# Latent attention: where the softmax is divided, and one norm chain for keys and queries

## Chip, cores and metric

One core of a Trainium2 chip runs the whole program. The metric is device time in microseconds from one launch; the kernel before was timed three times, and one further execution was profiled.

## What is computed

Two decoder blocks over 512 tokens of width 1024. The change lies in the second block's latent attention: 16 heads, of which each query and each key has 64 parts without and 32 parts with rotation. All four kinds are normalised by their mean square:

```python
c_kv = rms_norm_2(ckv[..., :KV_LORA_RANK], kv_a_norm)
k_rope = apply_rope(rms_norm_2(ckv[..., KV_LORA_RANK:], k_rope_norm), cos, sin)
kv = (c_kv @ w_kv_b).reshape(bsz, seq, N_HEADS, QK_NOPE_DIM + V_DIM)
k_nope = rms_norm_2(kv[..., :QK_NOPE_DIM], k_nope_norm)
...
q_nope = rms_norm_2(q[..., :QK_NOPE_DIM], q_nope_norm)
q_rope = apply_rope(rms_norm_2(q[..., QK_NOPE_DIM:], q_rope_norm), cos, sin)
...
s = jnp.einsum('bhqd,bhkd->bhqk', q_blk, k).astype(jnp.float32) * scale
s = jnp.where(key_pos[None, :] <= query_pos[:, None], s, NEG_INF)
p = jax.nn.softmax(s, axis=-1).astype(v.dtype)
return jnp.einsum('bhqk,bhkd->bhqd', p, v)
...
x = x + o @ mla_w_o[j]
```

## The kernel before

Every product of float32 matrices is made of three passes (`passes`): each operand is split into a high and a low part (`split`: ScalarE writes the high part, VectorE or GpSimd the rest).

The method `mla` works on four groups of four heads. For each group it makes keys (`k0` to `k3`), queries (`q0` to `q3`), values (`v0` to `v3`) and the output projection (`o0` to `o3`) in the order of `HEADS_ORDER`; these parts are generators, and after every step of attention the main loop takes as many pieces of them as `MLA_PACE` and `MLA_PIECES` say, so that projections of the next group run beside the attention of this one. `mla_tokens` projects keys or queries into `tok` (tokens on partitions), sums their squares into `m_ssq`, makes the factors `hs_s` by a chain of small VectorE instructions (`hs_m`, `rq_a`, `rq_y`), scales the 64 parts on GpSimd and the 32 parts on VectorE, and rotates the queries' 32 parts with `rope`. Keys get a copy of the one rotated key part, `krope`.

The attention has 32 units: for each head two units of two blocks of 128 queries. `mla_qk` transposes queries and keys of a head; `mla_probs` makes a unit's scores in PSUM (`ps_z`), adds the mask `wide` and takes the maximum in one VectorE instruction (`a_mx`), multiplies the maximum by minus the scale, lets ScalarE take the exponential with the sum (`a_sm`), and multiplies each row of probabilities `mp` by the reciprocal of its sum, one block on VectorE and one on GpSimd. Four units later (`MLA_AHEAD`) `mla_turn` transposes the probabilities on TensorE and splits them (`pth`, `ptl`), and after both heads of a pair `mla_out` calls `pair_out`: products with the values (`ps_s`), of which the upper 64 partitions hold what the values' low parts give, so that ScalarE copies them to `t`, VectorE adds the two halves of each head, and the result is split into `os`.

Engines take their instructions in a fixed order, set when the program is built; semaphores make one wait for another. PSUM has two banks for `ps_d` (projections), two for `ps_z`, three for `ps_p` (transposes) and one for `ps_s`. The tiles `t` have three buffers.

Of the kernel before, what the change touches and what calls it, by code (L numbers as in the profile page):

```python
# [16 lines left out]
P = 128  # L17
T = 512
# [30 lines left out]
MLA_PIECES = dict(k=7, q=7, v=5, o=8)  # L49
# [9 lines left out]
def shape_constants():  # L59
# [14 lines left out]
    wide[:, 3 * P:4 * P] = np.where(c > r, -BIG, 0.0)  # L74
# [55 lines left out]
class Kern:  # L130
# [104 lines left out]
    def pair_out(self, hi, lo, n, v, p):  # L235
# [60 lines left out]
    GUESS = {1: 0x5E82C800, 32: 0x6102C800}  # L296
# [84 lines left out]
    def load_constants(self):  # L381
# [21 lines left out]
        self.pad(self.cp, 16)  # L403
# [986 lines left out]
    def rope_tables(self):  # L1390
# [11 lines left out]
        for nm in ("q", "k"):  # L1402
            g = self.row(nm + "_rope")
            t = self.cp.tile([P, 4, 4, 16], F32, name="rope_" + nm)
            for i, (src, half) in enumerate(((w[2], 0), (w[1], 1), (w[1], 0), (w[2], 1))):
                gb = g[:, half * 16:half * 16 + 16].unsqueeze(1).to_broadcast(sh)
                self.tt(t[:, i], src, gb, ALU.mult)
# [3 lines left out]
    def rope(self, out, x, tab, sh):  # L1411

        n = math.prod(sh[1:])
        t = [self.tmp() for _ in range(-(-n // 128))]
        names = "abcd"[:len(sh) - 1]
        dims = {c: s for c, s in zip(names, sh[1:])}
        per = T // n
        t = [t[i // per][:, i % per * n:(i % per + 1) * n].rearrange(
            f"p ({' '.join(names)}) -> p {' '.join(names)}", **dims) for i in range(4)]
# [37 lines left out]
    def mla(self, x):  # L1457
# [21 lines left out]
        for c in range(4):  # L1479
# [5 lines left out]
        self.rope(krope, krt, lambda i: tabs["k"][:, i], [P, 4, 16])  # L1485
# [5 lines left out]
        copy_k = lambda x: nc.gpsimd.tensor_copy(out=x, in_=krope.unsqueeze(2).to_broadcast([P, 4, 4, 32]))  # L1491
        tab_q = lambda i: tabs["q"][:, i].unsqueeze(2).to_broadcast([P, 4, 4, 16])
        make = dict(k=lambda t: self.mla_tokens(t, st, lat["kv"], 64, copy_k),
                    v=lambda t: self.mla_values(t, st, lat["kv"]),
# [360 lines left out]
```

## Time and profile before

| what | value |
|---|---|
| three runs | 2255.79, 2259.34, 2263.17 us; median 2259.34 |
| profiled execution | 2261.87 us, span of the trace 2260.0 us |
| busy share of the span | TensorE 96%, VectorE 63%, ScalarE 44%, GpSimd 12% |
| mean granted TensorE clock | 0.981 of full speed |
| latent attention with its lead-in | about 1600 to 1890 us |

The names of engines in rows are PE (TensorE matmuls), PEld (its loads of weights), DVE (VectorE), ACT (ScalarE), POOL (GpSimd). An instruction of a helper has the helper's line: L205 is any two-operand VectorE or GpSimd instruction, L209 one with scalars, L212 one with a scalar and two operands, L215 any ScalarE instruction, L231 any matmul of `passes`; tiles tell them apart. A busy TensorE is not TensorE at its peak, since matmuls are pipelined.

### The profile page before, as it was taken

To read this page: it belongs to the slowest core of one execution; us is meant where nothing else is said; L and a number is where in the kernel's file an instruction comes from. 1 tells how busy PE (TensorE), PEld (TensorE's weight loads), DVE (VectorE), ACT (ScalarE), POOL (GpSimd) and SP (SyncE) were. 2 spreads that over 40 slices of the span, in tenths; PEclk is the share of its full clock that TensorE was granted. 3 is DMA by queue.
4 is the path that set the end of the run, shared out by engine and by line. 5 is a ranking of instruction groups with operands and counts; after the bars stand their busy time and mean duration, and the time that the engine had idled before them with its cause. 6 is when DMAs were issued, how large, how long until landed. Compare 5 with 4: busy or idle time off the path is not lost.

```text
span 2260.0 us, 28842 instructions
## 1 busy us (share of the span) xinstructions
PE 2161.9 (96%) x10586; PEld 1808.0 (80%) x10586; DVE 1416.0 (63%) x2778; ACT 1001.7 (44%) x1902; POOL 278.1 (12%) x308
## 2 busy tenths in 40 slices
PE   8998999999999999998789999999988999999999
PEld 7777878887888888887668788888777877888887
DVE  6678756667667656657884554354579886543542
ACT  5443346666444545454223432233467655432331
POOL 4123201111000000000440000000025441000000
PEclk9999999999999999999899999999999999999999
DMA  4211123235423343443663233232220111323322
GB/s 153 88 48 38 33 90 111 98 117 173 149 84 104 124 152 126 146 150 123 208 208 107 85 98 98 94 103 93 82 65 32 47 37 58 101 94 95 101 93 93
DMA packets 86829, 231.60 MB, mean 102 GB/s; under 512 B 10016, under 2 KB 19744, under 8 KB 86688
## 3 DMA queue, kind: packets, MB, share of 16 engines
q1 hardware_dynamic: 74016, 208.60, 28.5%
q10 hardware_dynamic: 12672, 21.16, 3.0%
q8 instruction: 83, 1.36, 0.2%
q14 instruction: 58, 0.48, 0.1%
HBM read 202.46 MB, written 27.26 MB: 102 GB/s over the span
## 4 chain that ended last, share of the span: by engine, by line
PE 81%; DVE 11%; ACT 3%; issue 2%; DMA 2%; POOL 1%; SPq 0%; ACTq 0%; DVEq 0%; POOLq 0%
PE ps_d L231 68%; PE ps_p L263 3%; PE ps_p L231 3%; PE ps_z L231 2%; PE ps_s L243 1%; DVE t L205 1%; DVE wlo L205 1%; PE ps_s L263 1%; DMA matB<-s5m 1%; PE ps_p L848 1%; ACT sb_e L215 1%; DVE h L212 0%; DVE s5t L205 0%; DVE mp L1646 0%; DVE tok L205 0%
## 5 line engine op out<-in xcount | busy, mean ns | idle before, releaser
L231 PE MATMUL ps_d<-h,whi 128*128 128x512 f32 (+1 forms) x3152 | 996.5, 393 | 9.9 <-DVE t L205 5.1
L215 ACT ACTIVATE whi<-wraw 128x512 fp32r<-128x512 f32 (+1 forms) x648 | 403.0, 625 | 722.4 <-PE ps_d L231 638.7
L231 PEld LDWEIGHTS ps_d<-h,whi 128*128 128x128 f32 (+1 forms) x3152 | 591.8, 189 | 134.5 <-ACT whi L215 4.9
L205 DVE TENSOR_TENSOR wlo<-wraw,whi 128x512 fp32r<-128x512 f32 x585 | 409.5, 703 | 381.2 <-ACT whi L215 375.8
L231 PE MATMUL ps_d<-h,wlo 128*128 128x512 f32 (+1 forms) x1576 | 620.3, 394 | 4.9 <-DVE wlo L205 4.9
L231 PEld LDWEIGHTS ps_d<-h,wlo 128*128 128x128 f32 (+1 forms) x1576 | 297.3, 189 | 66.9 <-DVE wlo L205 6.6
L231 PE MATMUL ps_d<-fh,whi 128*128 128x512 f32 x608 | 237.3, 390 | 0.0
L231 PE MATMUL ps_d<-fl,whi 128*128 128x512 f32 x608 | 237.0, 390 | 0.0
L231 PE MATMUL ps_d<-fh,wlo 128*128 128x512 f32 x608 | 236.6, 389 | 0.0
L205 DVE TENSOR_TENSOR t<-ps_d,rsb 128x512 f32<-128x512 f32 x136 | 92.9, 688 | 127.1 <-PE ps_d L231 124.2
L231 PEld LDWEIGHTS ps_d<-fl,whi 128*128 128x128 f32 x608 | 114.1, 188 | 23.7
L231 PEld LDWEIGHTS ps_d<-fh,wlo 128*128 128x128 f32 x608 | 114.2, 188 | 23.6
L231 PEld LDWEIGHTS ps_d<-fh,whi 128*128 128x128 f32 x608 | 114.1, 188 | 23.1
L205 POOL TENSOR_TENSOR wlo<-wraw,whi 128x512 fp32r<-128x512 f32 (+3 forms) x63 | 78.4, 1249 | 107.1 <-ACT whi L215 106.9
L215 ACT ACTIVATE fh<-t 128x512 fp32r<-128x512 f32 x76 | 47.9, 631 | 63.2 <-DVE t L205 54.4
L205 DVE TENSOR_TENSOR fl<-t,fh 128x512 fp32r<-128x512 f32 x76 | 52.6, 692 | 32.8 <-ACT fh L215 30.7
L231 PE MATMUL ps_d<-whi,c 128*128 128x256 f32 (+1 forms) x224 | 55.3, 331 | 12.5 <-DVE v L212 10.2
L1645 POOL MEMSET mp<- 128x128 f32 x32 | 6.6, 209 | 461.1 <-PE ps_d L231 444.8
L231 PEld LDWEIGHTS ps_d<-whi,c 128*128 128x128 f32 x224 | 39.7, 201 | 15.7 <-DVE v L212 11.6
L231 PE MATMUL ps_d<-os,whi 128*128 128x512 f32 x128 | 47.9, 428 | 4.1 <-ACT os L215 2.1
L215 ACT ACTIVATE t<-ps_d 128x512 f32<-128x512 f32 (+1 forms) x42 | 25.1, 597 | 58.3 <-PE ps_d L231 58.0
L205 DVE TENSOR_TENSOR x<-ps_d,x 128x512 f32<-128x512 f32 x56 | 38.3, 688 | 15.8 <-PE ps_d L231 15.6
(406 smaller groups left out, 3254.7 us busy)
## 6 DMA issues: line engine op xcount, KB each, us to landing
wraw<-in_w_gu SPq DMA_DIRECT2D x88, 512.0 KB, 3.3
wraw<-in_w_ff SPq DMA_DIRECT2D x64, 512.0 KB, 3.3
wraw<-in_w_dn SPq DMA_DIRECT2D x44, 512.0 KB, 3.4
wraw<-in_w_gates SPq DMA_DIRECT2D x24, 512.0 KB, 3.4
wraw<-in_w_glu SPq DMA_DIRECT2D x16, 512.0 KB, 3.3
wraw<-in_w_sc SPq DMA_DIRECT2D x12, 512.0 KB, 3.4
gsc<-t SPq DMA_DIRECT2D x24, 256.0 KB, 2.0
sg<-gsc SPq DMA_DIRECT2D x24, 256.0 KB, 3.5
```

What stands on the lines that cost most here:

```text
L205: self.note((eng or self.nc.vector).tensor_tensor(out=out, in0=a, in1=b, op=op))
L215: self.note(self.nc.scalar.activation(out, a, fn, **kw))
L231: self.note(self.nc.tensor.matmul(ps, lhsT=a, rhs=b, start=(start and n == 0), stop=(stop and n == 3 * len(ops) - 1), skip_group_check=loose))
L243: self.note(self.nc.tensor.matmul(o, lhsT=v(h, j), rhs=x, start=(j == 0 and i == 0), stop=(j == n - 1 and i == 1)))
L263: self.nc.tensor.matmul(ps, lhsT=lhsT, rhs=rhs, start=start, stop=stop)
L848: self.nc.tensor.matmul(self.sb_at(z, i), lhsT=self.tri if j == i else self.neg, rhs=self.sb_at(s, j), start=False, stop=(j == i and n == ...
L1645: nc.gpsimd.memset(p[b][:, c0 + n:c0 + n + P], 0.0)
```

## The change

Three things are done differently. (1) The queries' gain holds minus the scale (`qgain`), the mask is positive, and a row's least value is taken in place of its greatest, so that it is the bias of the exponential as it stands. (2) Probabilities are not divided. The sums of a pair of heads and two query blocks are kept in one tile; in `pair_out` VectorE takes the reciprocal of each sum spread over 64 columns, TensorE transposes that twice into a bank of `ps_p`, and VectorE multiplies the heads' outputs by it. (3) The latent's own norm factor no longer multiplies the head norms; it becomes an offset (`mla_offs`) of the mean square. Keys and queries of a group are first only projected (`mla_raw`), and one chain of 48 columns then serves both. The rotation takes two products over all 32 parts, where it had four over 16. `MLA_PIECES`, pads and tables follow.

```diff
-MLA_PIECES = dict(k=7, q=7, v=5, o=8)
+MLA_PIECES = dict(k=5, q=8, v=5, o=8)
...
-    wide[:, 3 * P:4 * P] = np.where(c > r, -BIG, 0.0)
+    wide[:, 3 * P:4 * P] = np.where(c > r, BIG, 0.0)
...
         self.act(s[0:64], po[64:128])
+        if sums is not None:
+            rc = self.tmp()[:, 0:256].rearrange("p (a h n) -> p a h n", a=2, h=2)
+            self.nc.vector.reciprocal(out=rc, in_=sums.unsqueeze(3).to_broadcast([P, 2, 2, 64]))
+            pr = self.ps("p")
+            for a in range(2):
+                self.nc.tensor.transpose(pr[:, a * P:(a + 1) * P], rc[:, a].rearrange("p h n -> p (h n)"), self.ident)
         y = self.tmp()[:, 0:256]
         for h in range(2):
             hs = slice(h * 256, h * 256 + 256)
             self.tt(y[h * 64:h * 64 + 64], po[0:64, hs], s[0:64, hs], ALU.add)
+        if sums is not None:
+            self.tt(y, pr[:, 0:256], y, ALU.mult)
         self.split(hi, lo, y)
...
-        x1, x2 = x[..., 0:16], x[..., 16:32]
-        self.tt(t[0], x1, tab(0), ALU.mult)
-        self.tt(t[1], x2, tab(1), ALU.mult)
-        self.tt(t[2], x1, tab(2), ALU.mult)
-        self.tt(t[3], x2, tab(3), ALU.mult)
-        self.tt(out[..., 0:16], t[0], t[1], ALU.subtract)
-        self.tt(out[..., 16:32], t[2], t[3], ALU.add)
+        t = [self.tmp()[:, 0:n].rearrange(f"p ({' '.join(names)}) -> p {' '.join(names)}", **dims) for _ in range(2)]
+        for i in range(2):
+            self.tt(t[i], x, tab(i), ALU.mult)
+        self.tt(out[..., 0:16], t[0][..., 0:16], t[0][..., 16:32], ALU.subtract)
+        self.tt(out[..., 16:32], t[1][..., 0:16], t[1][..., 16:32], ALU.add)
...
+        self.ts(self.qgain, self.col("qk_q"), -1.0 / math.sqrt(96), ALU.mult)
+        self.mla_offset(0, lat["kv"][1])
+
+        def make_k(g):
+            self.ssq = self.tmp("m_ssq", shape=[P, 3, 4, 4])
+            yield from self.mla_raw(heads[g]["k"], st, lat["kv"], 64, [self.ssq[:, 0]])
+
+        def make_q(g):
+            ssq = self.ssq
+            yield from self.mla_raw(heads[g]["q"], st, lat["q"], 96, [ssq[:, 1], ssq[:, 2]])
+            yield from self.mla_tokens(heads[g]["k"][0], heads[g]["q"][0], ssq, krope, tab_q)
...
+    def mla_offset(self, i, scale):
+        self.nc.vector.reciprocal(out=self.offs[:, i], in_=scale[1])
+        self.ts(self.offs[:, i], self.offs[:, i], 64 * EPS, ALU.mult)
+
+    def mla_raw(self, head, st, latent, nq, ssq):
...
+            for (lo, hi), out in zip(parts, ssq):
+                self.nc.vector.tensor_reduce(out=out[:, c, :], in_=sq[:, :, lo:hi], axis=AX.X, op=ALU.add)
             yield
+        head.append(tok)
+
+    def mla_tokens(self, k, q, ssq, krope, tab_q):
+        nc = self.nc
+        wide = lambda t, n: t.unsqueeze(3).to_broadcast([P, n, 4, 4])
+        m = self.tmp("hs_m", shape=[P, 3, 4, 4])
+        self.tt(m[:, 0:2], ssq[:, 0:2], wide(self.offs, 2), ALU.add)
+        self.stt(m[:, 2:3], ssq[:, 2:3], 2.0, wide(self.offs[:, 1:2], 1), ALU.mult, ALU.add)
+        y = self.rsqrt(m.rearrange("p i c h -> p (i c h)"), (P, 48), "h", k=8).rearrange(
+            "p (i c h) -> p i c h", i=3, c=4)
+        scaled = lambda i, w: y[:, i].unsqueeze(3).to_broadcast([P, 4, 4, w])
+        nc.gpsimd.tensor_copy(out=k[:, :, :, 64:96], in_=krope.unsqueeze(2).to_broadcast([P, 4, 4, 32]))
         yield
+        x = q[:, :, :, 64:96]
+        self.tt(x, x, scaled(2, 32), ALU.mult)
+        self.rope(x, x, tab_q, [P, 4, 4, 32])
         yield
+        for i, t in enumerate((k, q)):
+            x = t[:, :, :, 0:64]
+            self.tt(x, x, scaled(i, 64), ALU.mult, nc.gpsimd)
+        yield
...
             nc.vector.tensor_tensor_reduce(out=p[b][:, cs], in0=z[b][:, cs], in1=wide[:, 4 * P - n:], scale=1.0,
-                                           scalar=-3e38, op0=ALU.add, op1=ALU.max, accum_out=mx[:, a:a + 1])
-        self.ts(mx, mx, -sc, ALU.mult)
+                                           scalar=3e38, op0=ALU.add, op1=ALU.min, accum_out=mn[:, a:a + 1])
         for a, (b, cs) in enumerate(cols):
-            self.act(p[b][:, cs], p[b][:, cs], AF.Exp, scale=sc, bias=mx[:, a:a + 1], accum_out=sm[:, a:a + 1])
-        nc.vector.reciprocal(out=sm, in_=sm)
-        for a, (b, cs) in enumerate(cols):
-            self.ts(p[b][:, cs], p[b][:, cs], sm[:, a:a + 1], ALU.mult, eng=nc.gpsimd if a else None)
+            self.act(p[b][:, cs], p[b][:, cs], AF.Exp, scale=-1.0, bias=mn[:, a:a + 1], accum_out=sums[a])
         return p
```

The first place is on VectorE, where the second output tile of the first group is put together (`t<-ps_s,t` adds the halves). Before:

```order
L1651 RECIPROCAL a_sm<-a_sm 128x2
L1577 TENSOR_REDUCE m_ssq_15177<-tm 128x4
L209 TENSOR_SCALAR mp<-mp,a_sm 128x384
L205 TENSOR_TENSOR t<-ps_s,t 64x256 x2
L212 SCALAR_TENSOR_TENSOR qkl<-ps_p,cols,qkh 96x512
L205 TENSOR_TENSOR os<-t,os 128x256
```

and after:

```order
L249 RECIPROCAL t<-a_sm 128x256
L205 TENSOR_TENSOR t<-ps_s,t 64x256 x2
L1594 TENSOR_REDUCE m_ssq<-tm 128x4
L205 TENSOR_TENSOR t<-ps_p,t 128x256
L1594 TENSOR_REDUCE m_ssq<-tm 128x4
L212 SCALAR_TENSOR_TENSOR qkl<-ps_p,qgain,qkh 96x512
L205 TENSOR_TENSOR os<-t,os 128x256
```

The reciprocal of 256 columns stands directly ahead of the additions, and a product with the transposed reciprocals follows them.

The second place is on TensorE, at the third pair of query blocks and heads: projections for the next group (`ps_d<-whi,c`), scores (`ps_z`) and the transposes of the next unit's probabilities (`ps_p<-cst,mp`). Before:

```order
L231 MATMUL ps_d<-whi,c 128x384 x2
L231 MATMUL ps_d<-wlo,c 128x384
L231 MATMUL ps_z<-qkh 128x384
L231 MATMUL ps_z<-qkh,qkl 128x384
L231 MATMUL ps_z<-qkl,qkh 128x384
L231 MATMUL ps_z<-qkh 128x512
L231 MATMUL ps_z<-qkh,qkl 128x512
L231 MATMUL ps_z<-qkl,qkh 128x512
L1665 MATMUL ps_p<-cst,mp 128x128 x8
```

and after:

```order
L231 MATMUL ps_d<-whi,c 128x384 x2
L231 MATMUL ps_d<-wlo,c 128x384
L252 MATMUL ps_p<-cst,t 128x128 x2
L1680 MATMUL ps_p<-cst,mp 128x128 x8
L231 MATMUL ps_z<-qkh 128x384
```

The transposes of the reciprocals (L252) are new and stand right ahead of those of the probabilities, and the scores that stood ahead of these now stand behind them.

The third place is on GpSimd, around the scaling of the second group's keys and queries. Before, with the products of the probabilities between:

```order
L1491 COPY tok<-krope 128x16x32
L205 TENSOR_TENSOR wlo<-wraw,whi 128x384 x2
L1645 MEMSET mp 128x128
L209 TENSOR_SCALAR mp<-mp,a_sm 128x256
L1645 MEMSET mp 128x128
L209 TENSOR_SCALAR mp<-mp,a_sm 128x256
L205 TENSOR_TENSOR tok<-tok,hs_s_14909 128x16x64
```

and after:

```order
L1608 COPY tok<-krope 128x16x32
L205 TENSOR_TENSOR wlo<-wraw,whi 128x384 x2
L1664 MEMSET mp 128x128
L205 TENSOR_TENSOR tok<-tok,rq_yh 128x16x64 x2
L1664 MEMSET mp 128x128 x2
```

The products of the probabilities are gone, and the scalings of keys and queries stand next to each other.

## Rows read from the trace of the kernel before

**Rows 1.** Page, part 1: busy us, share of the span, instructions

```profile
PE 2161.9 (96%) x10586; PEld 1808.0 (80%) x10586; DVE 1416.0 (63%) x2778; ACT 1001.7 (44%) x1902; POOL 278.1 (12%) x308
```

**Rows 2.** Stretches: us, busy PE, PEld, DVE, ACT, POOL (count), clock, DMA, GB/s

```profile
1675.00:1885.00 210.00, 185.24 (x1125) 162.71 (x1126) 183.51 (x549) 137.67 (x337) 98.30 (x102) 0.93 0.12 39
1736.00:1760.00 24.00, 18.37 (x121) 16.31 (x120) 23.65 (x81) 15.40 (x39) 13.19 (x14) 1.00 0.06 17
1799.00:1816.00 17.00, 12.68 (x84) 10.91 (x83) 16.31 (x47) 11.41 (x27) 9.65 (x10) 0.90 0.20 62
```

**Rows 3.** Chain of waits, 1675 to 1885 us, shares by line

```profile
by line: PE ps_d L231 25.0%; PE ps_z L231 10.6%; PE ps_s L243 6.5%; DVE mp L1646 5.1%; DVE t L205 5.1%; DVE tok L205 4.9%; DVE ptl L205 4.8%; PE ps_p L1665 4.5%; PE ps_p L1613 3.9%; ACT mp L215 3.6%; issue 2.8%; DVE v L212 2.3%; DVE a_mx L2
```

**Rows 4.** Waits, 1680 to 1885 us: total us, times, longest

```profile
PE ps_d L231 <- DVE v L212: 9.4, 5, 3.1
DVE a_sm L1651 <- ACT mp L215: 3.6, 6, 1.3
```

**Rows 5.** VectorE groups, 1640 to 1900 us: busy us, mean ns | idle before

```profile
L209 DVE TENSOR_SCALAR mp<-mp,a_sm 128x384 f32<-128x384 f32 x16 | 8.1, 505 | 0.2
L209 DVE TENSOR_SCALAR mp<-mp,a_sm 128x128 f32<-128x128 f32 x16 | 5.0, 313 | 0.1
L209 DVE TENSOR_SCALAR a_mx<-a_mx 128x2 f32<-128x2 f32 x32 | 9.5, 298 | 0.1
L1651 DVE RECIPROCAL a_sm<-a_sm 128x2 f32<-128x2 f32 x32 | 5.3, 165 | 4.1 <-ACT mp L215 3.6
L212 DVE SCALAR_TENSOR_TENSOR hs_m<-m_ssq,ls_q 128x16 f32<-128x16 f32 x8 | 3.1, 408 | 0.0
L209 DVE TENSOR_SCALAR hs_m<-hs_m 128x32 f32<-128x32 f32 x4 | 2.6, 640 | 0.1
L212 DVE SCALAR_TENSOR_TENSOR rq_yh<-rq_ah,rq_yh 128x32 f32<-128x32 f32 x8 | 1.5, 188 | 0.1
L205 DVE TENSOR_TENSOR t<-tok,rope_q 128x256 f32<-128x256 f32 x16 | 6.4, 456 | 0.0
L205 DVE TENSOR_TENSOR x<-ps_d,x 128x512 f32<-128x512 f32 x32 | 21.7, 687 | 3.3 <-PE ps_d L231 3.1
L205 DVE TENSOR_TENSOR os<-t,os 128x256 fp32r<-128x256 f32 x16 | 6.6, 420 | 2.9 <-ACT os L215 2.9
L205 DVE TENSOR_TENSOR tok<-tok,hs_s 128x512 f32<-128x512 f32 x4 | 8.8, 2190 | 0.0
```

**Rows 6.** VectorE's other reciprocals, whole span

```profile
L474 DVE RECIPROCAL beta<-g_e 128x16 f32<-128x16 f32 x1 | 0.3, 253 | 0.0
L1117 DVE RECIPROCAL small<-small 128x32 f32<-128x32 f32 x1 | 0.4, 353 | 0.0
```

**Rows 7.** Timeline, GpSimd and VectorE: start us, us, what

```profile
1714.43 1.90 POOL L205 TENSOR_TENSOR tok<-tok,hs_s 128x1024 f32<-128x1024 f32 x1
1714.63 2.24 DVE L205 TENSOR_TENSOR tok<-tok,hs_s 128x512 f32<-128x512 f32 x1
```

**Rows 8.** GpSimd groups, 1640 to 1900 us

```profile
L209 POOL TENSOR_SCALAR mp<-mp,a_sm 128x512 f32<-128x512 f32 x16 | 26.4, 1651 | 18.0 <-DVE a_sm L1651 13.7 <-DVE a_mx L209 2.5 <-PE ps_d L231 1.7
L209 POOL TENSOR_SCALAR mp<-mp,a_sm 128x256 f32<-128x256 f32 x16 | 15.7, 981 | 22.3 <-DVE a_sm L1651 8.5 <-PE ps_d L231 4.9 <-DVE rq_yh L209 3.8
```

**Rows 9.** Chain of waits in order of time: start us, us, what

```profile
1736.80 0.43 DVE t L205
1774.67 1.42 ACT mp L215 x4
1795.44 3.16 PE ps_d L231 x18
1867.69 0.87 PE ps_p L1665 x8
1881.53 0.42 DVE t L205
```

**Rows 10.** TensorE's transposes of the probabilities, 1675 to 1885 us

```profile
L1665 PE MATMUL ps_p<-cst,mp 128*128 128x128 f32 x192 | 29.4, 272 | 0.0
```

More of the change, by code (lines that the diff above doesn't have):

```diff
@@ L233, in passes, with pair_out @@
                 n += 1
-    def pair_out(self, hi, lo, n, v, p):
+    def pair_out(self, hi, lo, n, v, p, sums=None):
         po = self.ps("s")
@@ L1490, in mla @@
         heads = [{} for _ in range(4)]
[L1491 to L1494, printed above, removed]
-                    q=lambda t: self.mla_tokens(t, st, lat["q"], 96, lambda x: self.rope(x, x, tab_q, [P, 4, 4, 16])))
+        tab_q = lambda i: tabs["q"][:, i].unsqueeze(2).to_broadcast([P, 4, 4, 32])
+        self.ts(self.qgain, self.col("qk_q"), -1.0 / math.sqrt(96), ALU.mult)
[7 more added lines that the diff above has]
+            yield from self.mla_tokens(heads[g]["k"][0], heads[g]["q"][0], ssq, krope, tab_q)
+        make = dict(k=make_k, q=make_q, v=lambda g: self.mla_values(heads[g]["v"], st, lat["kv"]))
         order = iter(HEADS_ORDER)
@@ L1503, in more @@
                 else:
-                    t = heads[g][part[0]] = []
-                    yield from make[part[0]](t)
+                    heads[g][part[0]] = []
+                    yield from make[part[0]](g)
                     yield
@@ L1525, in mla @@
                     qk[l % 2] = self.mla_qk(l, heads[g]["q"][0], heads[g]["k"][0])
-                live[n] = self.mla_probs(u, qk[l % 2], wide)
+                if l % 2 == 0:
+                    sums[l // 2, u] = self.tmp("a_sm", shape=(P, 2, 2), bufs=4)
+                live[n] = self.mla_probs(u, qk[l % 2], wide, [sums[l // 2, u][:, a, l % 2:l % 2 + 1] for a in range(2)])
             if n >= MLA_AHEAD:
@@ L1532, in mla @@
                 if l % 2:
-                    self.mla_out(l // 2, u, pt, heads[g]["v"], outs[g][l // 2])
+                    self.mla_out(l // 2, u, pt, heads[g]["v"], outs[g][l // 2], sums.pop((l // 2, u)))
                     pt = []
@@ L1559, in token_major @@
             yield c, o
-    def mla_tokens(self, head, st, latent, nq, rot):
-        nc = self.nc
-        cl, (r, r2) = latent
+    def mla_offset(self, i, scale):
+        self.nc.vector.reciprocal(out=self.offs[:, i], in_=scale[1])
+        self.ts(self.offs[:, i], self.offs[:, i], 64 * EPS, ALU.mult)
+    def mla_raw(self, head, st, latent, nq, ssq):
         tok = self.pool.tile([P, 4, 4, 96], F32, name="tok", tag="tok", bufs=4)
-        parts = [(0, 64)] if nq == 64 else [(0, 64), (64, 96)]
-        n = len(parts)
-        sh = [P, n, 4, 4]
-        ssq = self.tmp(f"m_ssq{n}", shape=sh)
-        for c, ps in self.token_major(st, cl, 4 * nq):
+        parts = [(0, 64), (64, 96)][:len(ssq)]
+        for c, ps in self.token_major(st, latent[0], 4 * nq):
             self.act(tok[:, c, :, 0:nq], ps.rearrange("p (h n) -> p h n", n=nq))
@@ L1609, in mla_qk @@
         qk = []
-        for src, gcol in ((q, "qk_q"), (k, "qk_k")):
+        for src, gc in ((q, self.qgain), (k, self.col("qk_k"))):
             pt = self.ps("p")
@@ L1624, in mla_place, with mla_probs @@
         return [(0, 0), (u, 256 * (1 - u))]
-    def mla_probs(self, u, qk, wide):
+    def mla_probs(self, u, qk, wide, sums):
         nc = self.nc
         (qh, ql), (kh, kl) = qk
-        sc = 1.0 / math.sqrt(96)
         nb = u + 1
@@ L1669, in mla_turn, with mla_out @@
         return hl
-    def mla_out(self, pair, u, hl, V, o):
+    def mla_out(self, pair, u, hl, V, o, sums):
         hi, lo = (t[:, u * 256:u * 256 + 256] for t in o)
@@ L1675, in mla_out @@
         self.pair_out(hi, lo, 2 * u + 2, lambda h, j: V[j][:, (2 * pair + h) * P:(2 * pair + h + 1) * P],
-                      lambda h, j: [at(t, j) for t in hl[h][j // 2]])
+                      lambda h, j: [at(t, j) for t in hl[h][j // 2]], sums)
     def dump_blocks(self, name, tiles):
```

46 lines of the change are left out of this document (12 added, 34 removed).

## Prediction

> **What bounds the kernel now.** I read the page first: TensorE is busy 96% of the span, VectorE 63% [rows 1], so anything that does not keep TensorE waiting is worth nothing. Then the busy times by stretch. The latent attention's pipelined part, 1675 to 1885 us, is the only place that the change touches in quantity, and there the reader sees another picture: TensorE 185.2 of 210 us, VectorE 183.5, ScalarE 137.7, GpSimd 98.3, granted clock 0.93 [rows 2]. In two stretches around the norms of the next heads VectorE is full: 23.65 of 24 us and 16.31 of 17, while TensorE has 18.4 and 12.7 [rows 2]. The chain of waits of the same 210 us says it again: the five TensorE lines it names make up 50.5%, ScalarE's exponentials 3.6%, issue 2.8%; VectorE lines make up most of the remaining 43% [rows 3]. So neither engine is the bound all along. A microsecond of VectorE work is worth about 0.45 us here (my choice, from that 43%); it is worth a whole one in the full stretches and nothing where TensorE is full. The waits show how VectorE holds TensorE up: TensorE sat 9.4 us until VectorE had evacuated the values, and VectorE itself sat 3.6 us in front of the reciprocal of the sums, because the exponentials were not done [rows 4].
>
> **What goes from VectorE.** The multiplications of the probabilities, 8.1 + 5.0 us; the 32 negations of the maxima, 9.5 us (298 ns each, where an undisturbed one would be near the 165 ns of the reciprocal of the same shape); that reciprocal, 5.3 us [rows 5]. Together 27.9 us. The norms had 26 small instructions per group of heads (12 for keys, 14 for queries) and have 11: 60 fewer over four groups. An undisturbed one costs some 0.18 us (the 188 ns row), which gives 10.6 us, and the first two rows of the chain carry a surcharge: 8 x (408 - 188) + 4 x (640 - 188) = 3.6 us [rows 5]. So 14.2 us. The rotation's sixteen 256-wide products (6.4 us) become eight 512-wide ones; at the 687 ns of a 512-wide instruction that is 5.5 us, 0.9 less [rows 5]. In all 43.0 us go.
>
> **What comes to VectorE.** Sixteen reciprocals of 128x256, which no row of before shows. The three reciprocal forms that it has are 165 ns for 2 elements, 253 for 16, 353 for 32 [rows 5, 6]: 6.25 ns for each further element, both times. That makes 353 + 224 x 6.25 = 1753 ns, and 28.0 us for sixteen. From below, an ordinary 256-wide instruction is 420 ns [rows 5], and sixteen of those would be 6.7 us; I take the line through its own three points. Sixteen products with the transposed reciprocals from PSUM, 256 wide, at 420 ns: 6.7 us. Two short reciprocals and two scalings for the offsets: 0.7 us. In all 35.4 us.
>
> The Trainium skill (VectorE: DVE Perf Modes, section "First, the fixed hardware budget") says that Reciprocal runs as an iterated divide with a repeat count of 8. That speaks against the wide reciprocal: at eight 0.96 GHz cycles for an element, an estimate from that page, it would be 2.13 us and sixteen would add 6 us more than my line; the rows' slope agrees in kind (six cycles) and not in size, so the sum goes by the rows.
>
> **The port.** One more VectorE term depends on GpSimd. At 1714.43 GpSimd starts to scale query parts (1.90 us), at 1714.63 VectorE starts a 512-wide product of two SBUF operands, and that takes 2.24 us in place of 0.69 [rows 5, 7]; all four such products average 2190 ns. Before, one such GpSimd instruction stands there for each group; after, two in a row (third place of the order shown above). Either VectorE gets in between and waits once, as now, or the first rotation product waits for the second GpSimd instruction as well: 4 x 1.9 = 7.6 us more. Or VectorE comes first and its product shrinks to 0.69: 6.0 us less. I take + 4. GpSimd loses 42.1 us of probability products [rows 8], which blocked VectorE's small instructions; that relief lies in the rows that go, and I count no more of it.
>
> The Trainium skill (SBUF — State Buffer, section "SBUF: two separate sides") calls it an exclusive lock between GpSimd and a VectorE instruction with two SBUF inputs: whoever starts first holds it to its end. The 2.24 us agree; by that rule alone the higher of my ends would hold.
>
> VectorE's balance is -43.0 + 35.4 + 4 = -3.6 us, between -13.6 and 0. At 0.45 that is **-1.6 us**.
>
> **What else moves.** VectorE no longer stands before an unfinished exponential, since the sums are wanted only units later: of the 3.6 us I take **-3.0**, for they lie in its full stretches (the 1.42 us at 1774.67 are on the chain [rows 9]). TensorE gets 32 transposes. One of that form is 272 ns [rows 10], but eight in a row take 0.87 us on the chain [rows 9], so 109 ns each: 3.5 us, half of it on the chain, **+1.8** (above: 8.7 if each stands alone).
>
> The new wait is the one to look at: the two transposes stand in TensorE's order right behind the weights' matmuls and right before the transposes of the next unit's probabilities (second place of the order). They wait for the reciprocal, which VectorE takes only just before the additions of the heads' halves (first place). Behind them stand the probability transposes, for these ScalarE and VectorE, and then the next value products. Of the sixteen pairs of additions eight are on the chain now, the first at 1736.80, the last at 1881.53 [rows 9]; at those VectorE is what is late. Counted in the changed order, between the last value product and the transposes TensorE has 27, 11, 16, 6, 10, 7, 13, 5, 12, 9, 6, 0, 11, 0, 1 and 0 other matmuls, at 3.16 us for 18 [rows 9] some 0.18 us each. Ten or more cover a reciprocal of 1.75 us; 5 to 9 leave 0.2 to 0.9 us, which I leave to VectorE's 26.5 us of idle time; the four with none or one stand at the end of the heads, where TensorE would wait up to 4 x 1.75 = 7 us. I take half, **+3.5**, since VectorE has less to do there. The last pair has no work beside it and gets the 0.42 us product on its way, **+0.4**. The probability products on GpSimd were covered by four units of lead, and no wait of TensorE names them: their going is worth nothing by itself. Pads, names, sign of the mask and the gain column cost nothing; the one added scaling of a column at the start is a small instruction of under 0.2 us beside loads.
>
> **Sum.** -1.6 - 3.0 + 1.8 + 3.5 + 0.4 = +1.1 us on the profiled execution's 2261.87, which stands 2.5 us over the median 2259.34 of the runs shown. On the median: 2260.4, forecast 2260.5. What a measurement of this kernel can tell from no change is 0.3%, 6.8 us.
>
> **Rivals.** *The work saved counts in full (0.28).* VectorE gets the port first and the reciprocals fall into its idle time. For it: 156 instructions go from the engine that fills the stretches in which TensorE waits. Against it: the reciprocals cost what the multiplications cost. Then -13.6 x 0.7 (full stretches and their neighbours) - 3.6 + 1.8 + 0.4 = -11 us: 2248.
>
> *TensorE waits for the reciprocal (0.28).* VectorE begins each reciprocal no earlier than TensorE ends its last value product, because it stands in VectorE's order behind evacuations that are late themselves. Then the nine places with fewer than ten matmuls cost 1.75 us less their cover: 0.7 + 0.5 + 0.9 + 0.2 + 0.7 + 3 x 1.75 + 1.6 = 9.9 us. With the balance at its upper end 0: 9.9 + 1.8 - 3.0 + 0.4 = +9 us, 2268, and more where VectorE is later still. It decides when the nine lose 0.8 us each. For it: VectorE is 87% busy, and at four places no matmul stands between. Against it: the idle time.
>
> *The trade is even (0.44), the forecast.* The change takes multiplications over 256 to 512 keys away and puts in their place a reciprocal spread over 64 copies of each sum; on VectorE the two cost about the same.
>
> **Numbers.** All of the lower ends together (balance -13.6 in full, -3.6, +0.4) give 2243, all upper ones (balance 0, 9.9 for the wait, 8.7 for the transposes, nothing from the exponentials) 2278; with one case in ten left out at either end the range is 2248 to 2273; the forecast's own is 2254 to 2267. Faster by over 0.3%: 0.28; within: 0.44; slower: 0.28.
>
> **What would show it.** The reciprocals at 1.7 to 1.8 us in VectorE's groups (0.42 would make the first rival right). VectorE's busy time in the stretch within 8 us of 183.5. Waits of TensorE's transposes of t for the reciprocal: some 4 us in total for the forecast, 10 or more for the second rival. No wait of VectorE for exponentials. The 512-wide query product still near 2.2 us, and the first rotation product above 1 us where GpSimd's second scaling is ahead of it. I am wrong if the granted clock of the stretch moves from 0.93 by more than 0.03, which no term here foresees, or if the stretch's length moves by more than 7 us.

## The result, and the profile after

The changed kernel takes 2277.42 us (median of 4 runs, 2275.04 to 2279.34), the kernel before 2259.74 in the same comparison: ratio 1.0078 with the interval 1.0059 to 1.0098. It is 17.6 us slower; the forecast was 2260.5, its range ended at 2273. The profiled execution took 2279.34 us, its span 2277.6.

**Where it is.** I paired TensorE's instructions of the two traces by form and order and took the median distance of their starts, in stretches of 20 us. From 1680 us those of after stand 1.8 us behind, from 1760 7.1, from 1840 13.4, from 1880 to the end 17.6. So 15.8 us arise in the attention's pipelined part, and nothing behind it. The 1.8 us ahead of it arise in the first 300 us, in instructions that the change leaves alone. The traces of the experiments with unmoved tiles stand between -3.8 and +2.2 when the attention begins, so single executions differ by that much. Busy times by stretch, after (they answer to [rows 2]), and the busy times of the whole program (beside [rows 1]):

```profile
1675.00:1885.00 210.00, 181.70 (x1092) 159.25 (x1093) 181.93 (x411) 130.92 (x324) 60.74 (x72) 0.92 0.12 37
1736.00:1760.00 24.00, 19.68 (x131) 16.99 (x129) 23.32 (x57) 17.92 (x44) 8.36 (x9) 1.00 0.07 23
```
```profile
PE 2170.6 (95%) x10618; PEld 1814.3 (80%) x10618; DVE 1426.5 (63%) x2649; ACT 1001.4 (44%) x1902; POOL 236.6 (10%) x276
```

In the same 210 us VectorE runs 411 instructions in place of 549 and is as busy as before; the clock is where it was. But these 210 us hold less of the work, since the stage now ends some 16 us later. Over the whole program VectorE runs 129 instructions fewer and is busy 10.5 us longer (1426.5 against 1416.0). VectorE's groups from 1640 to 1915 us, after (beside [rows 5]):

```profile
L249 DVE RECIPROCAL t<-a_sm 128x256 f32<-128x256 f32 x16 | 27.9, 1742 | 0.0
L205 DVE TENSOR_TENSOR t<-ps_p,t 128x256 f32<-128x256 f32 x16 | 6.7, 419 | 1.8 <-PE ps_p L252 1.3
L205 DVE TENSOR_TENSOR t<-tok,rope_q 128x512 f32<-128x512 f32 x8 | 11.5, 1462 | 0.1
L205 DVE TENSOR_TENSOR tok<-tok,rq_yh 128x512 f32<-128x512 f32 x4 | 7.2, 1788 | 0.1
L205 DVE TENSOR_TENSOR os<-t,os 128x256 fp32r<-128x256 f32 x16 | 8.6, 534 | 0.5 <-ACT os L215 0.5
```

The reciprocals and the products came out as worked out (1742 for 1753 ns, 419 for 420). The Trainium skill (VectorE: DVE Perf Modes, section "First, the fixed hardware budget") with its repeat count of 8 would have made them 2.13 us, the estimate of the prediction; the row decides. The reciprocals' idle time of 0.0 says that VectorE came to each of them straight from other work. The last three rows are instructions with two SBUF operands, in all 27.3 us where before had 21.8. Waits from 1680 to 1900 us, after (beside [rows 4]):

```profile
PE ps_d L231 <- DVE v L212: 14.1, 6, 4.3
PE ps_p L252 <- DVE t L249: 3.5, 3, 1.7
PE ps_p L252 <- DVE rq_ah L205: 1.3, 1, 1.3
PE ps_p L252 <- DVE rq_ah L212: 0.9, 1, 0.9
PE ps_p L1680 <- DVE t L205: 3.0, 3, 2.0
DVE t L205 <- PE ps_p L252: 2.9, 4, 1.0
ACT pth L215 <- PE ps_p L1680: 14.5, 15, 2.1
```

TensorE waits directly for the reciprocals 6.8 us: the 3.5, the two waits put down to `rq_ah` (both end 0.15 us after the end of a reciprocal), and 1.1 at the last pair, at 1900 us. Behind its waits stand more: the probability transposes (L1680) wait behind those of the reciprocals, and ScalarE waits 14.5 us for them, where before it waited 6.7 us (`ACT pth L215 <- PE ps_p L1665: 6.7, 6, 2.3`). The wait for the values' evacuation (first row) grew by 4.7 us. The chain of waits of after, 1850 to 1864 us (beside [rows 9]), shows how that runs:

```profile
1853.91 1.68 DVE t L249
1855.59 0.04 issue
1855.64 0.44 PE ps_p L252 x2
1856.07 0.89 PE ps_p L1680 x8
1856.96 0.02 issue
1856.98 0.69 DVE mp L1665
...
1860.86 0.68 DVE ptl L205
1861.54 1.67 DVE t L249
1863.21 0.14 issue
1863.35 0.41 PE ps_p L252 x2
```

VectorE's reciprocal, TensorE's two transposes, the eight of the probabilities, VectorE's evacuations, the next reciprocal: each hands over to the other. From the first reciprocal's start to the second's transposes (1853.91 to 1863.76 us) VectorE is busy 9.55 of 9.85 us, TensorE 7.44: it has scores and value products beside them, but waits 0.65 us for the first reciprocal and 1.12 for the second. Six of the sixteen reciprocals stand on the chain, with 10.0 us together.

### The profile page after: what moved, and what is told of

Its sections match the earlier page's. It is cut to its first block, busy times and chain, and to the rows that moved or that the text cites. A ratio compares the mean times of both kernels' runs of the same rounds, so it can differ in the third digit from the quotient of the medians.

```text
span 2277.6 us, 28732 instructions
## 1 busy us (share of the span) xinstructions
PE 2170.6 (95%) x10618; PEld 1814.3 (80%) x10618; DVE 1426.5 (63%) x2649; ACT 1001.4 (44%) x1902; POOL 236.6 (10%) x276
## 4 chain that ended last, share of the span: by engine, by line
PE 81%; DVE 11%; ACT 3%; issue 2%; DMA 2%; POOL 1%; SPq 0%; POOLq 0%; ACTq 0%; DVEq 0%
PE ps_d L231 68%; PE ps_p L271 3%; PE ps_p L231 3%; PE ps_z L231 2%; DVE t L205 1%; PE ps_s L271 1%; PE ps_s L243 1%; DVE wlo L205 1%; PE ps_p L1680 1%; PE ps_p L857 1%; PE ps_p L1633 1%; ACT sb_e L215 0%; DVE h L212 0%; DVE ptl L205 0%; DVE t L249 0%
## 5 line engine op out<-in xcount | busy, mean ns | idle before, releaser
L215 ACT ACTIVATE whi<-wraw 128x512 fp32r<-128x512 f32 (+1 forms) x648 | 403.5, 625 | 725.7 <-PE ps_d L231 646.9
L215 ACT ACTIVATE fh<-t 128x512 fp32r<-128x512 f32 x76 | 48.0, 631 | 63.0 <-DVE t L205 54.4
L231 PE MATMUL ps_d<-whi,c 128*128 128x256 f32 (+1 forms) x224 | 56.2, 333 | 12.5 <-DVE v L212 10.3
L231 PEld LDWEIGHTS ps_d<-whi,c 128*128 128x128 f32 x224 | 41.1, 208 | 16.1 <-DVE v L212 11.9
L215 ACT ACTIVATE t<-ps_d 128x512 f32<-128x512 f32 (+1 forms) x42 | 25.1, 597 | 58.4 <-PE ps_d L231 58.0
L205 DVE TENSOR_TENSOR x<-ps_d,x 128x512 f32<-128x512 f32 x56 | 38.2, 685 | 14.8 <-PE ps_d L231 14.6
```

The costliest lines, as they stand in the source:

```text
L205: self.note((eng or self.nc.vector).tensor_tensor(out=out, in0=a, in1=b, op=op))
L215: self.note(self.nc.scalar.activation(out, a, fn, **kw))
L231: self.note(self.nc.tensor.matmul(ps, lhsT=a, rhs=b, start=(start and n == 0), stop=(stop and n == 3 * len(ops) - 1), skip_group_check=loose))
```

## The experiments

Differences in us are ratio minus 1, times 2260; the intervals are 2 to 5 us to either side. "In the stage" is the distance of paired TensorE instructions behind the attention less that ahead of it; it comes from one trace of each kernel, and leaves out what differs ahead of the edited part. It is +15.8 for the change. The code shows the lines that matter; "..." stands for lines left out. Theory D: the division carries the loss; theory C: the common norm chain does.

**1. The division alone** on the kernel before (the hunks of `pair_out`, `mla_probs`, `mla_out` and the dictionary `sums`; L252 and L249 are as in after).

```diff
-        nc.vector.reciprocal(out=sm, in_=sm)
...
-            self.ts(p[b][:, cs], p[b][:, cs], sm[:, a:a + 1], ALU.mult, eng=nc.gpsimd if a else None)
...
+            self.nc.vector.reciprocal(out=rc, in_=sums.unsqueeze(3).to_broadcast([P, 2, 2, 64]))
...
+                self.nc.tensor.transpose(pr[:, a * P:(a + 1) * P], rc[:, a].rearrange("p h n -> p (h n)"), self.ident)
...
+            self.tt(y, pr[:, 0:256], y, ALU.mult)
```

> The kernel before with the second part alone: sums kept, probabilities not divided, the spread reciprocal, its two transposes and the product in the heads' outputs. Theory D (the division carries the loss: 16 reciprocals of 1.74 us on VectorE, TensorE's transposes behind them): +10 to +15 us, 2270 to 2275. Theory C (the common norm chain carries it): within 4 us of before.

2286.17 us, ratio 1.0109 [1.0094, 1.0124]: +24.6, in the stage +22.4. D holds, and more than the whole loss is here, more also than the 15 us that D had at most. Waits, 1675 to 1905 us:

```profile
PE ps_p L252 <- DVE t L249: 7.6, 5, 2.6
```

**2. The norm chain alone** (the hunks of `mla_offset`, `mla_raw`, `mla_tokens`, the closures and the piece counts).

```diff
-MLA_PIECES = dict(k=7, q=7, v=5, o=8)
+MLA_PIECES = dict(k=5, q=8, v=5, o=8)
...
+        for i, t in enumerate((k, q)):
...
+            self.tt(x, x, scaled(i, 64), ALU.mult, nc.gpsimd)
```

> The kernel before with the common norm chain alone (keys and queries projected raw, offsets, one chain of 48 columns, both GpSimd scalings behind each other), the narrow rotation kept. Theory D: within 4 us of before, 60 small instructions less against two GpSimd scalings in a row. Theory C: +8 to +15 us, 2268 to 2275, with VectorE's rotation products and outputs held up to 1.9 us by GpSimd.

2267.21 us, ratio 1.0026 [1.0016, 1.0036]: +5.9, in the stage +8.4, between the numbers of the two theories. Fewer VectorE instructions, and slower. Its VectorE timeline shows where:

```profile
1749.86 0.69 DVE L205 TENSOR_TENSOR tok<-tok,rq_yh 128x512 f32<-128x512 f32 x1
1750.52 2.08 DVE L205 TENSOR_TENSOR os<-t,os 128x256 fp32r<-128x256 f32 x1
1752.52 3.12 DVE L205 TENSOR_TENSOR t<-tok,rope_q 128x256 f32<-128x256 f32 x4
1755.56 0.75 DVE L205 TENSOR_TENSOR tok<-t 128x256 f32<-128x256 f32 x2
1756.23 0.47 DVE L212 SCALAR_TENSOR_TENSOR v<-ps_d,ls_kv,v 128x256 fp32r<-128x256 f32 x1
```

On GpSimd the two scalings run beside it; the wait behind it, from 1740 to 1760 us:

```profile
1750.32 4.03 POOL L205 TENSOR_TENSOR tok<-tok,rq_yh 128x1024 f32<-128x1024 f32 x2
```
```profile
PE ps_d L231 <- DVE v L212: 6.1, 1, 6.1
```

The 256-wide os takes 2.08 us in place of 0.42 and the rotation 3.12 in place of 1.42, both while GpSimd scales; the evacuation of the values stands behind them in VectorE's order, and TensorE waits 6.1 us for it. The longest such wait before was 3.1 [rows 4]. Of the 8.4 us in the stage 3.8 arise around this place, from 1748 to 1772 us; the rest is spread.

**3 and 5. Negative scores and wide rotation**, first with the new column making the small tiles 32 bytes longer, then with the pad cut so that every shared SBUF tile keeps its address.

```diff
-        self.pad(self.cp, 16)
+        self.qgain = self.cp.tile([P, 1], F32, name="qgain")
+        self.pad(self.cp, 15)
...
-                                           scalar=-3e38, op0=ALU.add, op1=ALU.max, accum_out=mx[:, a:a + 1])
-        self.ts(mx, mx, -sc, ALU.mult)
+                                           scalar=3e38, op0=ALU.add, op1=ALU.min, accum_out=mx[:, a:a + 1])
```

The fifth differs from the third by `self.pad(self.cp, 8)` alone.

> The kernel before with the negative scores (32 scalings of 298 ns less) and the wide rotation (eight products less) alone. Both theories: 0 to 6 us faster, 2254 to 2260, because 9.5 us and 0.9 us of VectorE work go and nothing comes.

> The parts of the change other than division and norms (least of the negative scores, one gain column, wide rotation), on the kernel before, with the small tiles padded so that every shared SBUF tile keeps the address that it has before. If the third run's loss came from the 32 bytes by which its tiles had moved, the phases ahead of the attention stand within 3 us of before and the whole is some 5 us faster, 2255 (9.5 us of negations and 0.9 of products go). If it came from the edit itself (the exponentials' bias, the wide products that wait for the port), the time stays at 2272 to 2277.

2277.34 us, ratio 1.0075 [1.0058, 1.0091], against 2257.18, ratio 0.9986 [0.9974, 0.9998], in the stage -2.7. The same work, 20 us apart by the addresses of tiles alone. The shifted one loses 12.1 us ahead of the attention, in phases whose instructions are unchanged. TensorE's commonest group from 200 to 1600 us, of before, the shifted and the aligned kernel:

```profile
L231 PE MATMUL ps_d<-h,whi 128*128 128x512 f32 x2097 | 664.1, 394 | 5.8 <-ACT whi L215 3.2 <-DVE t L205 1.9 <-ACT h L215 0.5
```
```profile
L231 PE MATMUL ps_d<-h,whi 128*128 128x512 f32 x2105 | 676.2, 398 | 5.7 <-ACT whi L215 3.2 <-DVE t L205 1.8 <-ACT h L215 0.7
```
```profile
L231 PE MATMUL ps_d<-h,whi 128*128 128x512 f32 x2100 | 665.7, 394 | 6.2 <-ACT whi L215 3.2 <-DVE t L205 1.9 <-ACT h L215 1.1
```

The matmuls of the group got 4 to 5 ns longer on average. The third run is thus no measure of the edit; the fifth is: -3.2 us, and it is the only kernel with the whole computation that is faster than before.

**4, 6 and 8. The reciprocal of the 4 sums, copied over the 64 columns**: in the changed kernel with a tile that moves others by 64 bytes (4), the same with addresses kept (6), and in the division alone (8).

```diff
-            self.nc.vector.reciprocal(out=rc, in_=sums.unsqueeze(3).to_broadcast([P, 2, 2, 64]))
+            small = self.tmp("a_rc", shape=(P, 2, 2))
+            self.nc.vector.reciprocal(out=small, in_=sums)
+            self.nc.vector.tensor_copy(out=rc, in_=small.unsqueeze(3).to_broadcast([P, 2, 2, 64]))
```

> The changed kernel with the reciprocal taken of the 4 sums of a row and then copied out over 64 columns each, so that 1.74 us on VectorE become some 0.17 and 0.3 to 0.4; all else as changed. Theory D: 8 to 14 us faster than the changed kernel, 2263 to 2269. Theory C: at most 4 us faster, 2273 to 2277.

> The changed kernel with the reciprocal taken of the 4 sums and copied over the 64 columns, at unchanged addresses: VectorE's 1.74 us become some 0.17 + 0.2 to 0.4. Work theory (VectorE has more work than before in a stretch in which it is short): about 16 x 1.2 = 19 us less of it at 0.45 to 0.7, so 8 to 13 us faster than the changed kernel, 2264 to 2269. Gate theory (TensorE's order is held behind anything that VectorE does between the last value product and the transposes): the gate gets shorter by 1.2 us at eight places, 9 us, about the same; the two are told apart by the next run. If neither holds (GpSimd, the norms), it stays at 2275 or more.

> The division alone on the kernel before with the reciprocal of 4 sums and a copy over the 64 columns. VectorE then has some 19 us less to do than in the first run, and 7 us less than before: work theory, 2262 or less. Gate theory: the transposes still wait for VectorE's place in the order, though for a shorter instruction: 2268 to 2276. Against both, if the loss is GpSimd's or ScalarE's timing (probabilities left undivided free their buffers later or earlier): above 2278.

4: 2272.07 us, ratio 1.0053 [1.0033, 1.0072], of which 7.3 us arise ahead of the attention, so it tells little. 6: 2269.02 us, 1.0034 [1.0022, 1.0045], 10 us less than the change; in the stage +9.9, 6 less. 8: 2264.78 us, 1.0013 [1.0004, 1.0023], 22 us less than the first; in the stage +5.0, 17 less. The eighth lies between its two theories, at neither's number. VectorE's groups of the eighth:

```profile
L251 DVE COPY t<-a_rc 128x256 f32<-128x256 f32 x16 | 6.1, 381 | 0.0
L250 DVE RECIPROCAL a_rc<-a_sm 128x4 f32<-128x4 f32 x16 | 2.8, 173 | 2.7 <-ACT mp L215 2.6
```

19 us of VectorE gone gave 17 to 22 us there, but 6 to 10 us in the whole change.

**7. The division without the gate** (TensorE's wait for the reciprocal): the transposes read the identity.

```diff
-                self.nc.tensor.transpose(pr[:, a * P:(a + 1) * P], rc[:, a].rearrange("p h n -> p (h n)"), self.ident)
+                self.nc.tensor.transpose(pr[:, a * P:(a + 1) * P], self.ident, self.ident)
```

> The division alone on the kernel before, as in the first run, but TensorE's 32 transposes read the constant identity in place of the reciprocals, which VectorE still takes, unread: the outputs are not divided by the sums. VectorE has the same work, TensorE the same transposes, and nothing of TensorE's waits for the reciprocal. Gate theory: at least 10 of the first run's 26 us come back, 2276 or less. Work theory: at most 4 come back, 2282 to 2287.

2280.36 us, ratio 1.0081 [1.0066, 1.0097]: 6.3 us less than the first, between the two theories' numbers. In the stage it is +21.6, only 0.8 less than the first; the other 4.7 us of the two traces' distance stand ahead of the attention, where their instructions are the same. So the gate is the smaller part, and whether it costs 1 us or 6 stays open. The waits for the reciprocal (7.6 us) are gone, but those for the values' evacuation are 14.8 us in place of 12.1: part of the waiting only moved.

**9. No division at all**, to price what the change removes.

```diff
-        nc.vector.reciprocal(out=sm, in_=sm)
-        for a, (b, cs) in enumerate(cols):
-            self.ts(p[b][:, cs], p[b][:, cs], sm[:, a:a + 1], ALU.mult, eng=nc.gpsimd if a else None)
```

> The kernel before without any division: the reciprocals of the sums (5.3 us of VectorE), the multiplications of the probabilities on VectorE (13.1 us) and on GpSimd (42.1 us) are left out, and nothing is put in their place, so the outputs are not divided by the sums. It gives the price of what the change removes. Price of the prediction (0.45 us for one of VectorE): 18.4 x 0.45 = 8.3, and 3.0 for the wait for the exponentials, so some 2250. If the multiplications lie in time that VectorE has to spare: 2258 or more, and then the division's +26 us of the first run is the price of the added part alone. If VectorE bounds the stage: 2243 or less.

2251.94 us, ratio 0.9961 [0.9948, 0.9974]: -8.8, in the stage -8.7. The removed work had about the price that I gave it.

**17 and 18. Transposes alone, products alone**, each on the ninth kernel.

```diff
+            pr = self.ps("p")
...
+                self.nc.tensor.transpose(pr[:, a * P:(a + 1) * P], self.ident, self.ident)
```
```diff
+            self.tt(y.rearrange("p (a n) -> p a n", a=2), self.ones.unsqueeze(1).to_broadcast([P, 2, P]),
+                    y.rearrange("p (a n) -> p a n", a=2), ALU.mult)
```

> The kernel without any division, with the 32 transposes of the change at their place, reading the identity, so that they wait for nothing, and with nothing that reads them: the outputs are not divided by the sums. Their time in TensorE's order alone: 32 x 0.11 = 3.5 us, half to all of it on the path, 2253.5 to 2255.5. If the sixteen further PSUM banks, of three that the probability transposes share, hold these up: 2257 or more.

> The kernel without any division, with the 16 products of 128x256 at their place, by a constant of ones in place of the transposed reciprocals, and without reciprocals and transposes: the outputs are not divided by the sums. 6.7 us of VectorE: at the prediction's 0.45, 2255; at the full price that the late reciprocals had, 2259; above 2260 if a product at this place holds up more than its own time.

2259.01 us (0.9996 [0.9987, 1.0006]) and 2259.01 us (0.9998 [0.9989, 1.0008]). Over the ninth, the transposes cost 7.9 us and the products 8.3 (in the stage 6.7 and 8.3). The first is the number expected if the further PSUM banks hold the others up, the second that of the full price. TensorE's group of the seventeenth, 1675 to 1890 us, and VectorE's of the eighteenth, 1640 to 1920 us:

```profile
L250 PE MATMUL ps_p<-cst 128*128 128x128 f32 x32 | 7.5, 291 | 0.5 <-DVE qkl L212 0.5
```
```profile
L205 DVE TENSOR_TENSOR t<-ones,t 128x256 f32<-128x256 f32 x16 | 8.4, 527 | 0.0
```

The transposes wait for next to nothing, and their cost is near their busy time of 7.5 us. The products here read two SBUF operands and are longer than the change's 419 ns; what carries over is that they cost about their whole length. The probability transposes' wait for their evacuation grew beside it, from 1.3 to 5.3 us (ps_p <- ptl); all three kinds of transposes share the three buffers of `ps("p")`. How much of the 7.9 is length and how much buffers, no run parts.

**13. The wide reciprocal one unit earlier.**

```diff
                 pt.append(self.mla_turn(u, live.pop(n - MLA_AHEAD)))
+                if l % 2 == 0:
+                    sums[l // 2, u] = self.mla_recip(u, sums[l // 2, u])
```

> The division alone on the kernel before, with the same sixteen 128x256 reciprocals, but each taken one unit earlier in VectorE's order (right after the evacuations of the probabilities of the pair's first unit) into a tile of its own. VectorE's amount of work is that of the first run (2286). Place theory: the reciprocals cost what other VectorE work costs, some 0.45 x 28 = 13 us, and the products 7: -8.7 + 13 + 7 = 11 us over before, 2270 to 2274. Amount theory: 2281 to 2287.

2274.95 us, ratio 1.0055 [1.0035, 1.0076]: +12.4, 12 us less than the first, with VectorE's instructions the same; in the stage +15.0, 7 less. That is 1 us above the place theory's numbers and 6 us below the amount theory's. The reciprocal also left the rotating tiles `t` for a tile of its own, and no run parts that from the place.

**10, 11 and 16. GpSimd in the norm chain**: a GpSimd copy of a rotated column ahead of the scalings, in the chain alone (10) and in the change (16); and the keys' scaling on VectorE (11, in the code against the second run).

```diff
+        nc.gpsimd.tensor_copy(out=self.tmp()[:, 0:1], in_=q[:, 3, 3, 95:96])
         for i, t in enumerate((k, q)):
```
```diff
-            self.tt(x, x, scaled(i, 64), ALU.mult, nc.gpsimd)
+            self.tt(x, x, scaled(i, 64), ALU.mult, nc.gpsimd if i else None)
```

> The common norm chain alone, as in the second run, with one added GpSimd instruction ahead of its two scalings, a copy of one column that the rotation has written: the scalings cannot start before VectorE's rotation has ended, so they cannot hold VectorE's products of two SBUF operands up there. Lock theory (the second run's 7 us are two GpSimd scalings in a row in place of one, which stretch VectorE's rotations): at least 4 of the 7 come back, 2260 to 2263. Order theory (the norms of keys and queries in one piece hold the evacuations of the values and the next weights up): the heads are ready some 2 us later, 2267 to 2271.

> The changed kernel with nothing altered but GpSimd's two scalings held back until the rotation has ended. Lock theory: the 5 us that this gave with the norm chain alone come back here too, 2271 to 2274. If in the whole change the wide reciprocals hide the lock: 2276 to 2279.

> The common norm chain alone with the scaling of the keys on VectorE, so that GpSimd has one scaling for each group as before, and VectorE four 128x1024 products more, at least 4 x 1.3 = 5 us. Lock theory: the rotation loses its surcharge, but the products come in: 2262 to 2266. Order theory: slower by what the products add, 2269 to 2274.

10: 2262.07 us, ratio 1.0008 [0.9998, 1.0018]; 16: 2272.99, 1.0055 [1.0037, 1.0074]; 11: 2264.68, 1.0021 [1.0011, 1.0032]; in the stage +1.3, +13.8 and +4.1. The numbers of 10 and 16 are those of the lock theory, but their traces refute that reading. Timeline of the tenth:

```profile
1710.70 4.21 POOL L205 TENSOR_TENSOR tok<-tok,rq_yh 128x1024 f32<-128x1024 f32 x2 [0.33 <-DVE rq_yh L212]
1717.47 0.19 POOL L1609 COPY t<-tok 128x1 f32<-128x1 f32 x1 [2.40 <-DVE tok L205]
```
```profile
1749.79 0.47 DVE L212 SCALAR_TENSOR_TENSOR v<-ps_d,ls_kv,v 128x256 fp32r<-128x256 f32 x1
1752.15 1.85 DVE L205 TENSOR_TENSOR os<-t,os 128x256 fp32r<-128x256 f32 x1
1753.92 2.38 DVE L205 TENSOR_TENSOR tok<-tok,rq_yh 128x512 f32<-128x512 f32 x1
```

The copy landed behind the scalings in GpSimd's order, held nothing back, and the products are as long as before it (the three groups 27.8 us, second run 28.0). What it did is move the order: the values are now evacuated at 1749.79, ahead of os, and TensorE's longest wait there is 2.8 us, not 6.1; from 1748 to 1772 us the tenth loses nothing on before, where the second lost 3.8 us. The eleventh does test the lock: the rotation's sixteen products fall from 12.5 to 6.5 us, VectorE takes 6.6 us of key products in, and the time falls by 1.2 us, within the two intervals. Its number is the lock theory's (2262 to 2266), but it took as much work in as it took surcharge out, and TensorE's longest wait for the values is still 5.6 us.

**12, 14 and 15. Repairs**: the small reciprocal with ScalarE's spread and experiment 5 (12), the same one unit earlier (14), and the change with that and the copy of 10 (15). The code is the twelfth's against the eighth.

```diff
-            self.nc.vector.tensor_copy(out=rc, in_=small.unsqueeze(3).to_broadcast([P, 2, 2, 64]))
+            self.act(rc, small.unsqueeze(3).to_broadcast([P, 2, 2, 64]))
```

> The kernel before with the division on the reciprocal of 4 sums, its spread over 64 columns by ScalarE in place of VectorE, and the negative scores and the wide rotation, but each part's own norms. VectorE has 43 - 14.2 - 6.7 - 2.6 = some 20 us less than before. From the runs so far: the small division +3, less 16 copies of some 0.3 us at a price of one (5 us), less 4 for the negation: 2254 to 2257, the fastest of all. If what VectorE does between the value products and the transposes decides, and not its amount: 2260 or more, since ScalarE's copy is a second station on the way.

> As the twelfth kernel (division by the reciprocal of 4 sums, spread by ScalarE, with negative scores and wide rotation), with the reciprocal and its spread one unit earlier. Place theory: 2252 without division, 3 less for the negation, 7 more for the products and 3 for transposes and small instructions: 2257 to 2260, against 2265 with the spread late. Amount theory: no difference, 2263 to 2267, since no work is taken away.

> The whole change with both mends: the reciprocal of 4 sums and its spread by ScalarE one unit earlier, and GpSimd's scalings behind the rotation. From the parts: the fourteenth kernel's 2257 to 2260 and 1 to 2 for the mended norm chain, so 2258 to 2262; the same as before, and 15 to 19 us faster than the change. If the parts do not add up: 2265 or more.

12: 2265.12 us, 1.0024 [1.0011, 1.0037]; 14: 2264.25, 1.0015 [1.0005, 1.0026]; 15: 2264.8, 1.0019 [1.0008, 1.0029]; in the stage +7.0, +3.6 and +3.7. None is faster than before, and none came to the number that I wanted of it. The mended change is 13 us faster than the change. My 2257 to 2260 for 14 had the products at 7 and transposes with small instructions at 3; with 17 and 18 the parts give -8.8 + 7.9 + 8.3 - 3.2 = +4.2, and +3.4 was measured. Once the reciprocal is small, these runs can tell no difference by its place (2.0 us between 12 and 14).

## Why the prediction was wrong

**The sum.** +1.1 was forecast, +17.6 came. Term by term, forecast against measured alone:
- What the division removes: 18.4 x 0.45 = 8.3 and the exponentials' 3.0, so -11.3. Measured -8.8 (9). Right in mechanism, and within the interval.
- The wide reciprocals with TensorE's wait for them: 28.0 x 0.45 + 3.5 = 16.1. First run less ninth, transposes and products: 24.6 - (-8.8 + 7.9 + 8.3) = 17.2, in the stage 16.0. Right in sum. How it parts is open: the wait is 6.3 by first less seventh, 0.8 in the stage, and the VectorE work the rest, 10.9 or 15.2.
- The wait itself, read from the change's trace, is 6.8 us, between the forecast and the rival's 9.9. At the four places with no matmul or one between it is 4.0 us (forecast 3.5). At the five with 5 to 9, which I left to VectorE's idle time, it is 2.8 us (0.9, 1.25 and 0.65 at three of them). **This step failed**: VectorE began none of the sixteen reciprocals out of idle time, so there was none to hide them in.
- The transposes: +1.8, from 109 ns each in runs of eight. Measured 7.9, near the upper end that I named (8.7, if each stands alone). **This step failed**: two in a row take 0.44 us on the chain of after, eight 0.89, and I had put only half of the time on the path. How much of the 7.9 is the shared buffers, no run parts.
- The products: 6.7 x 0.45 = 3.0, and 0.4 for the last pair. Measured 8.3 for 8.4 us (527 ns each with a constant from SBUF), a price of one, which is 6.7 for the change's own. **This failed too**: 0.45 is a mean over the stage, and the product stands between the value products and the heads' outputs.
- The norm chain with the port and offsets: (-14.2 + 4 + 0.7) x 0.45 = -4.3. Measured +5.9, in the stage +8.4. **The worst step.** The surcharge by GpSimd came (6.2 us in the chain alone, bound 7.6), and VectorE's busy time did not fall with its 56 instructions fewer (1418.7 us against 1416.0). And the chain's order put the lengthened products in front of the values' evacuation; the tenth run, with the same lengths in another order, was 4 us faster (7 in the stage). I had named what a wait would hold up for the division, and not for this part.
- Negation and wide rotation: -10.4 x 0.45 = -4.7. Measured -3.2. Right as a sum, though VectorE was not less busy (1416.7 us); the 512-wide products took 1.1 us each, not the 687 ns of a form with a PSUM operand.

**VectorE's balance.** Forecast -3.6 us, at most 0. The lengths of VectorE's instructions, added up over the program, fell by 2.3 us (1544.8 to 1542.5), near the forecast; but its busy time rose by 10.5. In the traces an instruction's record overlaps the next by up to some 0.08 us (in the second run's timeline 1755.56 + 0.75 ends behind 1756.23), in all 128.8 us before and 116.0 after. So the many small instructions that went were worth less than their lengths, at which I had priced them.

**What does not add up.** The three parts alone give 24.6 + 5.9 - 3.2 = 27.3, the whole 17.6. VectorE's busy time does not add up either: +20.9, +2.7 and +0.7 us alone, +10.5 in the whole. Making the reciprocals small gives 22 us in the division alone and 10 in the whole. That the other two parts left VectorE room is no reason, since alone they make it no less busy; the cause of the difference stays open, and with it how much each failed step weighs in the whole.

**The rivals.** TensorE's wait for the reciprocal was there (6.8 us in the trace) and its 2268 nearest, but it alone is not the loss: with the wait taken out the division still costs 18.3 us. That the saved work counts in full is refuted: VectorE's busy time did not fall by the 13.6 us of that rival, it rose.

**The signs that I named.** The reciprocals' length, the clock, the rotation product above 1 us and the missing wait for exponentials came as said. The query product took 1.79 us, not 2.2, and the TensorE wait of 6.8 us lay between the forecast's 4 and the rival's 10. VectorE's busy time in the fixed stretch came as said (181.9) and misled, since the stretch holds less work. The stage's length (+15.8) failed: none of the other signs looked at the order.

**Still open:** which order the norm chain would need, since no run held GpSimd back; and why the small reciprocal alone (8) costs 2.9 us (5.0 in the stage) when removal, transposes and products by themselves give 7.4 (6.4 in the stage) and its VectorE time comes on top.

## What to carry to other kernels

Where two engines hand work to and fro, price an added instruction by its place: between one engine's result and the other's next input it costs much of its length (products 8.3 of 8.4 us, reciprocals 17 of 28), a unit earlier less (the same reciprocals, in a tile of their own, 5 to 9 us). Few transposes or products at such a place are not hidden because their engine is idle elsewhere. And before a small edit is judged, check that it leaves the addresses of the other tiles alone.

## What the runs showed of the hardware

- A shift of SBUF tiles by 32 bytes made TensorE's 128x512 matmuls 4 to 5 ns longer (394 to 398 ns), 12 us ahead of the edited part; with the addresses restored the loss was gone. Why a shift does this, no run shows.
- VectorE's reciprocal is close to a line over all sizes seen: 165 ns for 2 elements, 173 for 4, 253 for 16, 353 for 32, 1742 for 256. A copy of the same 256 took 381 ns.
- GpSimd's 128x1024 products stretch VectorE's instructions of two SBUF operands several times over (a 128x256 one from 0.42 to 2.08 us), where the two products with a PSUM operand that ran beside them kept their length (410 and 417 ns).
- Small VectorE instructions are held up too. Before, the 18 negations of two elements that ran alone took 157 ns on average, the 14 beside a GpSimd instruction 478, up to 1312. The four longest stood beside weight splits, which the change leaves in place.
- Records of VectorE instructions overlap: with 129 instructions fewer the sum of their lengths fell by 2.3 us and the overlap by 12.8, so that VectorE was busy 10.5 us longer.
